# The output projection in half precision: high and low parts of both sides, one scale per 128 tokens

## The chip, the cores and the metric

One core of one Trainium2 chip runs the whole kernel. A core has five engines with queues of their own: TensorE (PE, matmuls into PSUM; its weight loads are shown apart as PEld), VectorE (DVE), ScalarE (ACT), GpSimd (POOL) and SyncE (SP, which here only issues transfers). Each works its queue in order; they wait for each other by semaphores. The metric is the time of one execution on the device in microseconds (us), as the median of several runs; lower is better.

## The reference

One decoder layer for 2048 tokens of width 1024 with two attention branches side by side. Only what matters here:

```python
proj = h @ w_in[l]                       # h: normalised, modulated x
qa, ka, va, fa, za, qb, kb, vb, zb = jnp.split(proj, split_points, axis=-1)
oa = forgetting_attention(qa, ka, va, fa + b_fgate[l])     # 8 heads of 64, causal
oa = oa * jax.nn.silu(za)
ob = sliding_window_sink_attention(qb, kb, vb, sinks[l])   # 8 heads of 64, window 128
ob = ob * jax.nn.silu(zb)
y = jnp.concatenate([oa, ob], axis=-1) @ w_out[l]          # (2048, 1024) @ (1024, 1024)
x = x + gate[:, None, :] * rms_norm(y, g_post[l])
```

The change is in the last matrix product, with `w_out` of 1024 x 1024, and in the normalisation behind it. A scale per token in front of the normalisation cancels in `y / rms(y)`, apart from the small constant under the root.

## The kernel before

The kernel keeps fp32 accuracy on a half-precision matrix unit by splitting: a number is written as a high part plus a low part, and a product takes three matmuls (high x high, high x low, low x high). The stages, in order of time:

1. Start: modulation vectors, first tiles of x, rotary tables.
2. Input projection, in units of three matmuls. A list of such units (`punits`) is worked off in small portions between the steps of the attention; tasks that belong to a certain unit hang in `events`.
3. The sliding-window branch (roughly 206 to 455 us): 64 windows, one per pair of heads and 128-token block. Each iteration of the loop over `windows` transposes the last window's probabilities (PE), takes exponentials (ACT), scores of the next window (PE), their maxima (DVE) and the product with the values (PE), with projection units in between.
4. The other branch ("fox"): 8 heads x 20 steps, each step with scores (PE), two exponentials (ACT), a low part (DVE) and the product with the values (PE). Inside the last head (`hd == 7`) the output projection is prepared: `open_out` makes room, `w_out_load` and `w_out_split` bring `w_out` in sixteen pieces and split each into a high part (ACT, L1247) and a low part (DVE, L1248), scaled by one factor per 128 rows (`facs`).
5. Output projection: 16 tiles of 128 tokens (`class Out`), the first two inside the last head, 14 after it.

One tile of stage 5: `load` brings the attention output (128 tokens x 1024) and the gate (`z`, kept transposed). `turn(h)` transposes four 128x128 blocks on PE into one PSUM bank (L1271), multiplies them by the gate on DVE (L1275), copies the result into a high part on ACT (L1276) and takes the low part on DVE (L1277). High and low parts of both sides are of type `F32R`, a four-byte format that PE multiplies in one pass. `product(n, k)` issues three matmuls for a half `n` of the 1024 columns and a block `k` of the 1024 rows (L1290); sixteen such units make a tile. When a half is complete, ACT sums its squares (`yj`, L1299) and DVE multiplies it by the gate vector (`yg`, L1300). After the second half, `store` makes the reciprocal root of the mean square with one-column operations on DVE (L1309, then L93 to L104), and a last product and sum over 128x1024 (L1312), and sends the tile out.

Two things set the order. `after(n, f)` puts `f` off by `n` ticks, and in stage 5 `tick2` makes a tick after every second unit. And PSUM: three banks, `bk`, are handed out in turn by `bank()`; a half of a tile holds one while it is summed, and the transposes take the others. The units of a tile, with the turns of the next tile between them:

```python
for q in range(16):
    ounits.append(lambda t=t, q=q: outs[t].product(q // 8, q % 8))
    if t + 1 < NB and q in (4, 7):
        ounits.append(lambda t=t, q=q: outs[t + 1].turn(int(q == 7)))
```

Of the kernel before, what the change touches and what calls it, by code (L numbers as in the profile page):

```python
# [11 lines left out]
F32R = mybir.dt.float32r  # L12
# [29 lines left out]
def hybrid_layer(  # L42
# [103 lines left out]
    snk = const.tile([P, 8], F32, name="snk")  # L146

# [101 lines left out]
    scl, isc, czs, facs, kaps = {}, {}, {}, {}, {}  # L249
# [4 lines left out]
    def w_done(key):  # L254

        kind, j = key[:2], key[2:]
        pw = pws[key]
        if kind == "qk":
            kap = kappa(pw, key)
            scl[key] = col(f"scl_{key}")  # L260
            V.tensor_scalar(scl[key][:], kap[:], kap[:], 0.125, op0=ALU.mult, op1=ALU.mult)
            isc[key] = col(f"isc_{key}")
            V.reciprocal(isc[key][:], scl[key][:])
        elif kind == "qb":
            kap = kappa(pw, key)
            scl[key] = col(f"scl_{key}")
            V.tensor_scalar(scl[key][:], kap[:], kaps["kb"][:], 0.125, op0=ALU.mult, op1=ALU.mult)
        elif kind == "va":
            kaps[key] = kappa(pw, key)
        else:  # L270
            czs[key] = col(f"cz_{key}")
            V.tensor_scalar(czs[key][:], pw[:], pH[:], 2.0 ** -29, op0=ALU.mult, op1=ALU.mult)
            facs[key] = col(f"fac_{key}")
            V.tensor_tensor(facs[key][:], kaps["vb" if kind == "zb" else f"va{j}"][:], czs[key][:], op=ALU.mult)
# [722 lines left out]
    with swa_order:  # L997
# [6 lines left out]
        ps_pv = swa_pool("ps_pv", 1, space=PSUM)  # L1004
        base = N_PRO
# [6 lines left out]
        for n, wd in enumerate(windows):  # L1012
# [14 lines left out]
            if n >= 2:  # L1027
                windows[n - 2].pv()
        windows[NW - 1].turn()
# [9 lines left out]
        tick()  # L1039
    swa.close()  # L1040
# [186 lines left out]
    def open_out():  # L1227
# [6 lines left out]
        oio["w"] = wo.tile([P, 2, KT, D], F32R, name="wohl")  # L1234
# [8 lines left out]
    def w_out_split(m):  # L1243
        k, cc = m // 2, slice((m % 2) * CH, (m % 2 + 1) * CH)
        fac = facs[f"za{k}" if k < 4 else f"zb{k - 4}"]
# [6 lines left out]
    class Out:  # L1252
# [13 lines left out]
        def turn(self, h):  # L1266

            px = bk[bank()][:].rearrange("p (k n) -> p k n", k=4)
            ks = slice(4 * h, 4 * h + 4)
            for k in range(4):  # L1270
                PE.transpose(px[:, k, :], self.o[:, (4 * h + k) * P:(4 * h + k + 1) * P], ident[:])  # L1271
            if h == 0:
                self.hl = [wpool.tile([P, KT, P], F32R, tag=tag, name=f"oz_{tag}") for tag in ("wraw", "whl")]
            hi, lo = self.hl[0][:, ks, :], self.hl[1][:, ks, :]
            after(1, lambda: V.tensor_tensor(self.z[:, ks, :], px, self.z[:, ks, :], op=ALU.mult))  # L1275
            after(2, lambda: A.activation(hi, self.z[:, ks, :], AF.Copy))  # L1276
            after(3, lambda: V.tensor_tensor(lo, self.z[:, ks, :], hi.bitcast(F32), op=ALU.subtract))  # L1277

        def product(self, n, k):
# [9 lines left out]
            for m_, (i, j) in enumerate(((0, 0), (0, 1), (1, 0))):  # L1289
                PE.matmul(py, self.hl[i][:, k, :], w_slot(8 * j + k)[:, cc],  # L1290
# [16 lines left out]
        def store(self):  # L1307
            ss, y = self.ss, self.y
            V.tensor_tensor(ss[:, 0:1], ss[:, 0:1], ss[:, 1:2], op=ALU.add)  # L1309
            rst = sm(1, "y_rs")  # L1310
            rsqrt_mean(rst, ss[:, 0:1], 1)
            V.scalar_tensor_tensor(y[:], y[:], rst[:], self.x[:], op0=ALU.mult, op1=ALU.add)  # L1312
            SP.dma_start(os_[self.t * P:(self.t + 1) * P, :], y[:])
# [13 lines left out]
    def ofill(n, each=None):  # L1327
        for _ in range(n):
            n_, q = divmod(opos[0], 18)
# [7 lines left out]
    with tc.manual_schedule():  # L1337
# [23 lines left out]
        for s, stp_ in enumerate(steps):  # L1361
# [4 lines left out]
            if hd == 7 and r >= 8:  # L1366
                npn, fil = N_IN * (r - 7) // (NS - 8) - opos[0], ofill
# [41 lines left out]
            if hd == 7 and r == 6:  # L1409
                outs[0].turn(0)  # L1410
                outs[0].turn(1)
# [52 lines left out]
```

## Time and profile before

| | |
|---|---|
| median of 3 runs | 1290.12 us (1289.17 to 1294.97) |
| profiled execution, its own time | 1293.69 us |
| its span, first to last instruction | 1292.0 us |
| mean granted PE clock | 0.98 |
| busy: PE, DVE, ACT, POOL | 1212.4, 925.5, 686.6, 156.7 us |

A row of the timeline or of the chain gives start and duration in us, engine, line of the kernel, operation, output<-inputs with partitions x elements and type; in brackets stands how long the engine had been idle before it and what released it. A row of the windows gives the stretch, its length, then for PE, PEld, DVE, ACT and POOL the busy time and the number of instructions, then the granted PE clock, the share of the transfer engines and GB/s. A group's row ends with busy time, mean ns of one, and idle time before. PE's matmuls are pipelined, so their durations overlap: what counts there is the distance from start to start.

### The profile page before, as it was taken

What the parts mean: (1) busy time and instruction counts of PE and PEld (TensorE: products, weight loads), DVE (VectorE), ACT (ScalarE), POOL (GpSimd) and SP (SyncE); (2) the same over time, 40 slices, a digit from 0 to 9 for tenths busy, and PEclk for the clock granted to TensorE, in tenths of its full rate; (3) what the DMA queues carried; (4) which work ended last, traced back from release to release, by engine and by line L of the source; (5) the groups of instructions that cost most, each with busy time, mean ns of one, the idle gap of its engine ahead of it and who ended that gap; (6) DMA issues with size and microseconds to landing.
All of it is one profiled execution on the core that took longest, in us unless ns stands there. A gap on an engine that the chain in (4) does not pass through costs nothing. (4 is left out here: it accounts for less than half of the span.)

```text
span 1292.0 us, 27969 instructions
## 1 busy us (share of the span) xinstructions
PE 1212.4 (94%) x11171; PEld 779.8 (60%) x11171; DVE 925.5 (72%) x2290; ACT 686.6 (53%) x1085; POOL 156.7 (12%) x284
## 2 busy tenths in 40 slices
PE   5788999999999999999999999999999969999997
PEld 2366545765558966555555555555555637777875
DVE  6666677686877637678878787877777886656655
ACT  2665435454545432666766676676767786322121
POOL 2001133233333310010010100000000000000000
PEclk9889999999999999999999999999999979999999
DMA  9345321213221322133142322122111154354442
GB/s 331 135 121 150 78 81 54 63 45 85 66 77 42 38 62 64 44 89 74 49 61 74 87 58 67 44 68 40 38 42 42 38 175 127 115 193 162 164 164 81
DMA packets 81909, 115.85 MB, mean 90 GB/s; under 512 B 26956, under 2 KB 57716, under 8 KB 81780
## 3 DMA queue, kind: packets, MB, share of 16 engines
q1 hardware_dynamic: 70292, 81.05, 20.6%
q0 software_dynamic: 11488, 33.03, 10.5%
q8 instruction: 87, 1.43, 0.5%
q14 instruction: 42, 0.34, 0.1%
HBM read 66.84 MB, written 25.18 MB: 71 GB/s over the span
## 5 line engine op out<-in xcount | busy, mean ns | idle before, releaser
L1124 DVE TENSOR_REDUCE a_m<-bk 128x1 f32<-128x512 f32 (+2 forms) x320 | 191.1, 606 | 102.0 <-PE bk L1120 68.9
L1173 ACT ACTIVATE p<-sta,lift,scl_qk 128x1024 f32<-128x1024 f32 (+2 forms) x160 | 171.9, 1075 | 94.7 <-DVE pha L1180 83.3
L294 PE MATMUL bk<-hT,wh_qk 128*128 128x512 f16 x768 | 201.8, 378 | 0.1
L1177 ACT ACTIVATE pha<-sta,lift,scl_qk 128x1024 f16<-128x1024 f32 (+2 forms) x160 | 171.7, 1073 | 0.9
L1180 DVE TENSOR_TENSOR pha<-p,pha 128x1024 f16<-128x1024 f32 (+2 forms) x160 | 168.8, 1055 | 0.7 <-ACT pha L1177 0.7
L1290 PE MATMUL bk<-wohl,oz_wraw 128*128 128x512 f32 x512 | 166.8, 407 | 0.2 <-DVE T L1275 0.2
L1120 PE MATMUL bk<-T 66*128 66x512 f16 (+2 forms) x320 | 111.8, 350 | 13.2 <-DVE a_m L1124 7.3
L1166 PE MATMUL sta<-T 128*128 128x512 f16 (+1 forms) x320 | 112.6, 352 | 7.5 <-ACT pha L1177 7.2
L1193 PE MATMUL poa<-vt,pha 128*128 128x65 f16 x1088 | 116.7, 193 | 1.3 <-DVE pha L1180 1.3
L1192 PE MATMUL poa<-vt,pha 128*128 128x64 f16 x1088 | 117.1, 195 | 0.0
L1190 PE MATMUL poa<-vt,pha 128*128 128x65 f16 x1088 | 117.1, 193 | 0.1
L1190 PEld LDWEIGHTS <-pha 128*128 128x128 f16 x1088 | 101.6, 97 | 20.1 <-issue 5.3
L294 PEld LDWEIGHTS <-wh_qk 128*128 128x128 f16 x768 | 70.5, 97 | 69.3 <-issue 2.6
L1167 PE MATMUL sta<-T 69*128 69x512 f16 (+1 forms) x320 | 111.3, 353 | 0.0
L1192 PEld LDWEIGHTS <-pha 128*128 128x128 f16 x1088 | 101.4, 97 | 15.0 <-issue 0.2
L1290 PEld LDWEIGHTS bk<-wohl,oz_wraw 128*128 128x128 f32 x512 | 93.5, 189 | 22.8 <-DVE T L1275 2.6
L294 PE MATMUL bk<-hT,wh_za 128*128 128x512 f16 x384 | 103.5, 378 | 0.9 <-DVE a_m L1124 0.9
L1193 PEld LDWEIGHTS <-pha 128*128 128x128 f16 x1088 | 101.5, 99 | 1.4 <-DVE pha L1180 1.4
L1290 PE MATMUL bk<-wohl,oz_whl 128*128 128x512 f32 x256 | 101.6, 397 | 0.0
L312 PE MATMUL bk<-wh_va,hT 128*128 128x128 f16 x1536 | 96.2, 219 | 1.1 <-issue 0.8
L294 PE MATMUL bk<-hT,wh_zb 128*128 128x512 f16 x384 | 93.7, 380 | 2.0 <-DVE wh_zb L238 2.0
L312 PEld LDWEIGHTS <-hT 128*128 128x128 f16 x1536 | 88.9, 98 | 9.9 <-issue 7.6
(649 smaller groups left out, 2067.1 us busy)
## 6 DMA issues: line engine op xcount, KB each, us to landing
wa<-in_w_ada_dram SPq DMA_DIRECT2D x16, 512.0 KB, 10.1
z_d<-tz POOLq DMA_DIRECT2D x32, 256.0 KB, 2.8
T<-stq SPq DMA_DIRECT2D x128, 64.0 KB, 2.0
T<-o_d SPq DMA_DIRECT2D x16, 512.0 KB, 5.0
T<-z_d SPq DMA_DIRECT2D x16, 512.0 KB, 5.7
xr<-in_x_dram SPq DMA_DIRECT2D x16, 512.0 KB, 4.2
out_dram<-yg SPq DMA_DIRECT2D x16, 512.0 KB, 3.0
xt<-in_x_dram SPq DMA_DIRECT2D x12, 512.0 KB, 7.3
```

The lines of the kernel that those rows point to most:

```text
L294: PE.matmul(ps, whl[:, a, k, :], hT[ci][:, b, k, :], start=(k == 0 and n == 0), stop=(k == KT - 1 and n == 2))
L312: PE.matmul(ps[:, u * P:(u + 1) * P], hT[ci][:, a, k, u * P:(u + 1) * P], whl[:, b, k, :], start=(k == 0 and n == 0), stop=(k == KT - 1 an ...
L1120: PE.matmul(mx[:, :w], T[0:XM, 0, i * P:(i + 1) * P], T[0:XM, 2, pc * CH:pc * CH + w], start=True, stop=pc < ci)
L1124: V.tensor_reduce(m3[:, u, pc:pc + 1], mx[:, :w], axis=AX.X, op=ALU.max)
L1166: PE.matmul(self.st[:, o:o + w], T[:, 3, kb_], T[:, 1, qc], start=True, stop=False)
L1173: A.activation(self.p32[:, :self.w], self.st[:, :self.w], AF.Exp, scale=scl[f"qk{self.hd}"][:], bias=lift[:])
L1177: A.activation(self.ph[:, 0, :self.w], self.st[:, :self.w], AF.Exp, scale=scl[f"qk{self.hd}"][:], bias=lift[:])
L1180: V.tensor_tensor(self.ph[:, 1, :self.w], self.p32[:, :self.w], self.ph[:, 0, :self.w], op=ALU.subtract)
L1190: PE.matmul(po[:, u, :], ph[:, 0, pq], vt[:, b, hd, 0:65], start=(self.first and n == 0 and u == 0), stop=False)
L1192: PE.matmul(po[:, u, 0:64], ph[:, 0, pq], vt[:, b, hd, 65:VW], start=False, stop=False)
L1193: PE.matmul(po[:, u, :], ph[:, 1, pq], vt[:, b, hd, 0:65], start=False, stop=(self.last and n == len(self.blocks) - 1))
L1290: PE.matmul(py, self.hl[i][:, k, :], w_slot(8 * j + k)[:, cc], start=(k == 0 and m_ == 0), stop=(k == KT - 1 and m_ == 2))
```

## The change

- Both sides of the output projection are kept as `F16` high and low parts in place of `F32R`; the three matmuls per unit stay.
- `F16` has a narrow range, so both sides get a scale. For each tile of 128 tokens it comes from the sum of squares of the gated, transposed tile: Square with a row sum on ACT (`squares_`), a matmul against ones on PE that adds over the partitions, and `root_scale`, two integer operations on DVE that make about a reciprocal root (`scale_`). High and low parts are then made of the whole tile at once with this scale.
- For `w_out` the sum of squares is taken during the windows of stage 3: each iteration loads a 128x128 block of `w_out` on SP's queue and squares the block of the iteration before on ACT; every 16th iteration, and at the end, DVE reduces. At the end of the stage a matmul against ones and `root_scale` give `wrt`. In `open_out` it is combined with the eight factors (now columns of `fac8`) into `wsc`, the scale of each 128 rows, and `ysc`.
- `store` takes the scales out again: four more one-column operations. The reciprocal root, for its part, has two operations in place of four in each of its three steps for a single column, and one more before them.
- A tile's eight transposes are issued together, into two banks, after the third product unit of the tile before, where they were two groups of four after the fifth and the eighth.
- Inside the last head the first tile's turn puts its scale off by three ticks, later tiles by four (`lag`); the products start one step later (r = 9), and a tile with a turn counts 17 units in place of 18.

The diff, cut to its core:

```diff
 def rsqrt_mean(dst, ss, n):
...
+        V.tensor_scalar(v[:], v[:], -0.5, None, op0=ALU.mult)
         for it in range(3):
             t = sm(n, "rs_t")
-            V.tensor_tensor(t[:], y[:], y[:], op=ALU.mult)
-            V.tensor_tensor(t[:], t[:], v[:], op=ALU.mult)
-            V.tensor_scalar(t[:], t[:], -0.5, 1.5, op0=ALU.mult, op1=ALU.add)
+            if n == 1:
+                V.scalar_tensor_tensor(t[:], y[:], y[:], v[:], op0=ALU.mult, op1=ALU.mult)
+            else:
+                V.tensor_tensor(t[:], y[:], y[:], op=ALU.mult)
+                V.tensor_tensor(t[:], t[:], v[:], op=ALU.mult)
             y2 = dst if it == 2 else sm(n, "rs_y")
-            V.tensor_tensor(y2[:], y[:], t[:], op=ALU.mult)
+            V.scalar_tensor_tensor(y2[:], t[:], 1.5, y[:], op0=ALU.add, op1=ALU.mult)
             y = y2
+
+    def root_scale(dst, ss):
+        h = small.tile([P, 1], I32, tag="rs_h", name="sc_h")
+        V.tensor_scalar(h[:], ss.bitcast(I32), 1, None, op0=ALU.logical_shift_right)
+        V.tensor_scalar(dst.bitcast(I32), h[:], -1, 0x5F3759DF + (15 << 23), op0=ALU.mult, op1=ALU.add)
...
# loop over the windows, at the end of iteration n
+            if n:
+                A.activation(wsq[n - 1][:], wsq[n - 1][:], AF.Square, accum_out=wss[:, (n - 1) % 16:(n - 1) % 16 + 1])
+            if n and n % 16 == 0:
+                V.tensor_reduce(wst[:, n // 16 - 1:n // 16], wss[:], axis=AX.X, op=ALU.add)
+            wsq[n] = wsp.tile([P, P], F32, tag="wsq", name="wsq")
+            SP.dma_start(wsq[n][:], w_out0[n // 8 * P:(n // 8 + 1) * P, n % 8 * P:(n % 8 + 1) * P])
...
# after the last window
+        A.activation(wsq[NW - 1][:], wsq[NW - 1][:], AF.Square, accum_out=wss[:, 15:16])
+        V.tensor_reduce(wst[:, 3:4], wss[:], axis=AX.X, op=ALU.add)
+        wsum = sm(1, "w_mx2")
+        V.tensor_reduce(wsum[:], wst[:], axis=AX.X, op=ALU.add)
+        pw_ = bk[bank()][:, 0:1]
+        PE.matmul(pw_, ones[:], wsum[:], start=True, stop=True)
+        root_scale(wrt[:], pw_)
...
-        oio["w"] = wo.tile([P, 2, KT, D], F32R, name="wohl")
+        oio["w"] = wo.tile([P, 2, KT, D], F16, name="wohl")
...
-        A.activation(hi, raw[:], AF.Copy, scale=fac[:])
-        V.scalar_tensor_tensor(w_slot(8 + k)[:, cc], raw[:], fac[:], hi.bitcast(F32), op0=ALU.mult, op1=ALU.subtract)
+        A.activation(hi, raw[:], AF.Copy, scale=wsc[:, k:k + 1])
+        V.scalar_tensor_tensor(w_slot(8 + k)[:, cc], raw[:], wsc[:, k:k + 1], hi, op0=ALU.mult, op1=ALU.subtract)
...
-        def turn(self, h):
...
+        def turn(self, lag):
+            px = [bk[bank()][:].rearrange("p (k n) -> p k n", k=4) for _ in range(2)]
+            for k in range(KT):
+                PE.transpose(px[k // 4][:, k % 4, :], self.o[:, k * P:(k + 1) * P], ident[:])
+            self.hl = wpool.tile([P, 2, KT, P], F16, tag="whl", name="oz")
+            self.sc = sm(1, "w_pw")
+            hi, lo = self.hl[:, 0], self.hl[:, 1]
+            gs = sm(1, "w_mx")
+
+            def gate():
+                for h in range(2):
+                    z = self.z[:, 4 * h:4 * h + 4, :]
+                    V.tensor_tensor(z, px[h], z, op=ALU.mult)
+
+            def squares_():
+                junk = wpool.tile([P, KT, P], BF16, tag="wraw", name="zj")
+                A.activation(junk[:], self.z, AF.Square, accum_out=gs[:])
+
+            def scale_():
+                pg = bk[bank()][:, 0:1]
+                PE.matmul(pg, ones[:], gs[:], start=True, stop=True)
+                root_scale(self.sc[:], pg)
+
+            after(1, gate)
+            after(2, squares_)
+            after(lag, scale_)
+            after(lag + 1, lambda: A.activation(hi, self.z, AF.Copy, scale=self.sc[:]))
+            after(lag + 2, lambda: V.scalar_tensor_tensor(lo, self.z, self.sc[:], hi, op0=ALU.mult, op1=ALU.subtract))
...
# store
+            inv = sm(1, "w_sw")
+            V.tensor_tensor(inv[:], self.sc[:], ysc[:], op=ALU.mult)
+            V.reciprocal(inv[:], inv[:])
             V.tensor_tensor(ss[:, 0:1], ss[:, 0:1], ss[:, 1:2], op=ALU.add)
+            V.tensor_scalar(ss[:, 0:1], ss[:, 0:1], inv[:], inv[:], op0=ALU.mult, op1=ALU.mult)
             rst = sm(1, "y_rs")
             rsqrt_mean(rst, ss[:, 0:1], 1)
+            V.tensor_tensor(rst[:], rst[:], inv[:], op=ALU.mult)
...
-            if t + 1 < NB and q in (4, 7):
-                ounits.append(lambda t=t, q=q: outs[t + 1].turn(int(q == 7)))
+            if t + 1 < NB and q == 2:
+                ounits.append(lambda t=t: outs[t + 1].turn(4))
...
-    N_IN = 2 * 18
+    N_IN = 2 * 17
...
             if hd == 7 and r >= 8:
-                npn, fil = N_IN * (r - 7) // (NS - 8) - opos[0], ofill
+                npn, fil = N_IN * (r - 8) // (NS - 9) - opos[0], ofill
...
             if hd == 7 and r == 6:
-                outs[0].turn(0)
-                outs[0].turn(1)
+                outs[0].turn(3)
```

More of the change, by code (lines that the diff above doesn't have):

```diff
@@ L11 @@
 F32 = mybir.dt.float32
-F32R = mybir.dt.float32r
 F16 = mybir.dt.float16
@@ L146, in hybrid_layer @@
     snk = const.tile([P, 8], F32, name="snk")
+    fac8 = const.tile([P, KT], F32, name="fac8")
+    wrt = const.tile([P, 1], F32, name="wrt")
+    wsc = const.tile([P, KT], F32, name="wsc")
+    ysc = const.tile([P, 1], F32, name="ysc")
     def kappa(pw, name):
@@ L248, in hybrid_layer @@
     pws = {}
-    scl, isc, czs, facs, kaps = {}, {}, {}, {}, {}
+    scl, isc, czs, kaps = {}, {}, {}, {}
     def col(name):
@@ L272, in w_done @@
             V.tensor_scalar(czs[key][:], pw[:], pH[:], 2.0 ** -29, op0=ALU.mult, op1=ALU.mult)
-            facs[key] = col(f"fac_{key}")
-            V.tensor_tensor(facs[key][:], kaps["vb" if kind == "zb" else f"va{j}"][:], czs[key][:], op=ALU.mult)
+            n = int(j) + (4 if kind == "zb" else 0)
+            V.tensor_tensor(fac8[:, n:n + 1], kaps["vb" if kind == "zb" else f"va{j}"][:], czs[key][:], op=ALU.mult)
     def pieces(key):
@@ L1004, in hybrid_layer @@
         ps_pv = swa_pool("ps_pv", 1, space=PSUM)
+        wsp = swa_pool("wsp", 2)
+        wss = swa_pool("wss", 1).tile([P, 16], F32, name="wss")
+        wst = sm(4, "wst")
+        wsq = {}
         base = N_PRO
@@ L1233, in open_out @@
         stp = foxo.enter_context(tc.tile_pool(name="stpo", bufs=3, reuse_waits="tile"))
-        oio["w"] = wo.tile([P, 2, KT, D], F32R, name="wohl")
+        oio["w"] = wo.tile([P, 2, KT, D], F16, name="wohl")
+        fm = sm(1, "w_p2")
+        V.tensor_reduce(fm[:], fac8[:], axis=AX.X, op=ALU.max)
+        V.reciprocal(fm[:], fm[:])
+        V.tensor_tensor(ysc[:], wrt[:], fm[:], op=ALU.mult)
+        V.tensor_scalar(wsc[:], fac8[:], ysc[:], None, op0=ALU.mult)
     w_raw = {}
@@ L1264, in load @@
             SP.dma_start(self.z, z_d[:, :, rows_].rearrange("k p n -> p k n"))
-        def turn(self, h):
[L1268 to L1277, printed above, removed]
+        def turn(self, lag):
[22 more added lines that the diff above has]
+            after(lag + 2, lambda: V.scalar_tensor_tensor(lo, self.z, self.sc[:], hi, op0=ALU.mult, op1=ALU.subtract))
         def product(self, n, k):
@@ L1289, in product @@
             for m_, (i, j) in enumerate(((0, 0), (0, 1), (1, 0))):
-                PE.matmul(py, self.hl[i][:, k, :], w_slot(8 * j + k)[:, cc],
+                PE.matmul(py, self.hl[:, i, k, :], w_slot(8 * j + k)[:, cc],
                           start=(k == 0 and m_ == 0), stop=(k == KT - 1 and m_ == 2))
@@ L1328, in ofill @@
         for _ in range(n):
-            n_, q = divmod(opos[0], 18)
+            n_, q = divmod(opos[0], 17)
             if q == 0 and n_ + 2 < NB:
```

1 line of the change is left out of this document (removed).

## The prediction

> **What bounds the kernel now.** I read the windows by stage first, then the chain that ended last, then the timeline of one 128-token tile of the output projection. The windows show TensorE (PE) busy nearly all the time in that last stage, at full clock, while ACT idles and DVE works 62% of it:
>
> ```profile
> 1180.00:1220.00 40.00, 39.80 (x182) 31.78 (x181) 24.92 (x73) 8.79 (x21) 0.00 (x0) 1.00 0.55 183
> ```
>
> So time is won where a tile's work on PE gets shorter, and lost where PE waits. From the chain, the first transpose group of six consecutive tiles:
>
> ```profile
> 1201.21 0.44 PE bk L1271 x4
> ...
> 1262.69 0.44 PE bk L1271 x4
> ```
>
> The two rows are five tiles apart: (1262.69 - 1201.21)/5 = 12.30 us a tile. One tile in the timeline:
>
> ```profile
> 1209.85 0.63 PE L1290 MATMUL bk<-wohl,oz_wraw 128*128 128x512 f32 x2
> ...
> 1210.83 0.69 DVE L1300 TENSOR_TENSOR yg<-bk,gacc 128x512 f32<-128x512 f32 x1 [2.70 <-ACT yj L1299]
> ...
> 1211.44 0.15 DVE L1309 TENSOR_TENSOR y_ss<-y_ss 128x1 f32<-128x1 f32 x1
> ...
> 1214.50 1.28 DVE L1312 SCALAR_TENSOR_TENSOR yg<-yg,y_rs,xr 128x1024 f32<-128x1024 f32 x1
> ...
> 1215.70 0.68 DVE L1275 TENSOR_TENSOR T<-bk,T 128x512 f32<-128x512 f32 x1
> ...
> 1216.44 0.30 PEld L1290 LDWEIGHTS bk<-wohl,oz_wraw 128*128 128x128 f32 x2 [0.19 <-DVE T L1275]
> ...
> 1216.47 0.64 ACT L1276 ACTIVATE oz_wraw<-T 128x512 fp32r<-128x512 f32 x1 [5.67 <-issue]
> ...
> 1217.01 0.39 PE L1290 MATMUL bk<-wohl,oz_whl 128*128 128x512 f32 x1
> ...
> 1221.91 0.39 PE L1290 MATMUL bk<-wohl,oz_whl 128*128 128x512 f32 x1
> ```
>
> Take the tile's first matmul, 1209.85, as time 0. DVE starts the previous tile's store at +1.59, needs 16 one-column operations until +4.65 (3.06/16 = 0.19 us each), then the 1.28 us row product, and only then, at +5.85, the first gating product (L1275) of the next tile: DVE runs in order, and the store stands ahead of it. PE already waits for that gating product, 0.19 us, since it holds the bank that the second half of columns needs. From 1217.01 to 1221.91 lie seven units of three matmuls: 0.70 us a unit, 0.233 a matmul. Sixteen units are 11.2 us; the other 1.1 are two groups of transposes and this wait.
>
> **The products in half precision.** The input projection's matmuls of the same 128x512 shape are already f16:
>
> ```profile
> 283.04 2.12 PE L294 MATMUL bk<-hT,wh_zb 128*128 128x512 f16 x9
> ...
> L294 PE MATMUL bk<-hT,wh_qk 128*128 128x512 f16 x768 | 201.8, 378 | 0.1
> ```
>
> Nine take 2.12 us, the last one's 0.38 included: (2.12 - 0.38)/8 = 0.217 each, 0.65 a unit. A tile's 48 save 48 x 0.016 = 0.8 us. That is all that the number format can bring, as products stay three. The Trainium skill ("TensorE: Matmul & The Clock Gate", Back-to-back issue gap) has about 131 ns for a sustained 512-column matmul in a stream with weight loads. By it a unit would be 0.39 us; the row of nine denies it, and the row decides.
>
> **Eight transposes at once** take the place of two groups of four, and stand after three units instead of five and eight. Twenty in a row:
>
> ```profile
> 44.41 2.35 PE L377 MATMUL px<-ident,xt 128*128 128x128 f32 x20
> ```
>
> A transpose more costs (2.35 - 0.3)/19 = 0.11 us; with the 0.44 of a group of four, eight cost 0.88, as much as two groups. Nothing is gained or lost there. With them a tile without waits is 16 x 0.65 + 0.9 = 11.3 us.
>
> **The scale per 128 tokens** adds a chain of four engines. Gate both halves (DVE), sum the squares of the whole tile (ACT), add over partitions with a matmul against ones (PE), two column operations (DVE), high part (ACT), low part (DVE). The matmul sits in PE's queue four ticks after the turn; a tick comes every second unit and a tile has 17, so it stands, tile about, after the ninth or the tenth product unit. All later units of the tile queue behind it, and DVE's next work behind its two column operations. When is its input ready?
>
> ```profile
> 42.44 1.06 ACT L359 ACTIVATE junk<-hT 128x1024 bf16<-128x1024 f32 x1
> 43.40 0.19 ACT L359 ACTIVATION_READ_ACCUMULATOR junk<-hT 128x1 f32 x1
> ...
> 47.97 0.38 PE L602 MATMUL bk<-bm,ones 1*128 1x1 f32 x2 [0.37 <-DVE bm L601]
> 48.28 0.10 PEld L294 LDWEIGHTS <-wh_kb 128*128 128x128 f16 x1
> 48.39 0.16 DVE L87 TENSOR_SCALAR p2t<-bk 128x1 f32<-128x1 f32 x1 [0.47 <-PE bk L602]
> ```
>
> The store keeps its length: four column operations are added for undoing the scales, five of the reciprocal root go, 15 instead of 16, and four of the 15 now read a column as their scalar, which is dearer (0.23 in the first row below against 0.15 for a plain one): the two roughly cancel. Store and gate fall in the same tick, store first, as before. So gating starts at +5.85 again; both halves are now issued together, the second 0.61 later (the step from 1210.83 to 1211.44), ending at +6.46 + 0.68 = +7.14. ACT follows 0.09 later (1216.38 to 1216.47): +7.23. The same Square over 128x1024 takes 0.96 until its accumulator is read, and 0.19 for that: +8.38, and with a handover PE starts the matmul at +8.45. Nearest row for it is the ones matmul L602: 0.31 until the next weight load, and about 0.1 until the products run at pace: 0.4. DVE reads its result 0.42 after its start (47.97 to 48.39).
>
> ```profile
> 49.34 0.23 DVE L609 TENSOR_SCALAR Gp<-gcol,ipH 128x8 f32<-128x8 f32 x1
> ...
> L232 ACT ACTIVATE wh_qk<-wr_qk,w_sw 128x1024 f16<-128x1024 f32 x8 | 9.1, 1141 | 2.6 <-DVE w_sw L224 1.6 <-PE bk L294 0.9
> ```
>
> PE, unhindered, would be there at 9 x 0.65 + 0.88 = +6.7, or +7.4 after ten units. So it waits 1.7 or 1.1 us in all (some of it already at the bank of the first gating product, free at +6.53). A tile then takes 8.45 + 0.4 + seven units (4.55) = 13.4, or with six units 12.75: mean 13.1, against 12.3. The saving of the format is spent and 0.8 us more. What follows the matmul is hidden: 0.4 until DVE has it and 0.4 for the scale, 1.14 high part, 1.28 low part end by about +12.8 with ACT's and DVE's other work between, and the next tile needs the low part only with its third matmul.
>
> The last stage holds 14 tiles, 13 of them with a turn: 13 x 0.8 = +10.4; the last tile has none and saves 0.8. After its last matmul the chain is the store's, 15 operations for 16: nothing. The two tiles worked off inside the last attention head save 96 x 0.016 = 1.5 and pay two ones matmuls, 0.8; starting them a step later moves their work by one unit. I take -0.7, from -3 to +2, since that stretch waits on several engines.
>
> **The scale for w_out** is summed in the sliding-window stage: per window a 64 KB load on SP's queue and a Square of 128x128 on ACT.
>
> ```profile
> sum 249.00, PE 246.63 PEld 167.23 DVE 180.81 ACT 124.40 POOL 82.76; mean PE 61.66 PEld 41.81 DVE 45.20 ACT 31.10 POOL 20.69
> L735 ACT ACTIVATE vb<-bk 128x128 f16<-128x128 f32 x16 | 3.5, 273 | 2.5 <-PE bk L727 2.4
> ...
> 303.22 0.19 ACT L829 ACTIVATION_READ_ACCUMULATOR sm__4001<-sm__4001,b_nb 128x1 f32 x1
> 303.31 0.57 ACT L847 ACTIVATE ptb<-pxb 128x512 f16<-128x512 f32 x1
> ...
> 307.03 0.64 PE L838 MATMUL pxb<-ident,sm__4001 128*128 128x128 f32 x4
> ...
> 307.25 0.68 DVE L843 TENSOR_TENSOR ptb<-pxb,ptb 128x512 f16<-128x512 f32 x1
> ...
> T<-stq SPq DMA_DIRECT2D x128, 64.0 KB, 2.0
> ```
>
> At 0.27 + 0.19 each, 64 add 30 us to ACT, which is busy 124 of the stage's 249 us; PE is busy 247. Behind the square in ACT's queue stand the next exponentials and copies; PE reads an exponential 3.6 us after ACT finished it (303.41 to 307.03) and DVE takes a copy 3.4 us after its end (303.88 to 307.25). A delay of 0.46 stays inside. A 64 KB load lands in 2.0 us and has a window of 3.9 us (249/64); SP's rotations queued behind it wait for ACT anyway. I take 0; 0 to +4, and 30 were the cover gone.
>
> Its end is exposed. A matmul against ones closes the stage in PE's queue, behind two DVE reductions that stand behind DVE's last evacuation:
>
> ```profile
> 463.68 0.62 PE L1087 MATMUL bk<-identh,lq 128*69 128x128 f16 x8
> ...
> 464.17 0.76 DVE L321 SCALAR_TENSOR_TENSOR vt<-bk,vt 128x256 f16<-128x256 f32 x2
> ```
>
> DVE is free at 464.93, the reductions take 0.4, the matmul 0.4: the first of the bias rows (L1087, now 463.68) starts near 465.8, and the row copies on ACT and the projections behind them move by 2.1 us.
>
> **Sum:** 10.4 - 0.8 - 0.7 + 2.1 = +11.0 us. The profiled execution took 1293.69 us for a span of 1292.0; so 1304.7 for such a one. The median of the runs is 3.6 lower, 1290.12: predicted 1301.1.
>
> **Rivals.** *The sum is there in time (faster).* The wait is gone if the squares are summed by +6.7 to +7.4 instead of +8.45, that is if DVE reaches the gating 1.7 us earlier. Against it: the order store, gate in DVE's queue, and 1215.70. For it: only that four of the one-column operations could run in DVE's gaps before +1.59, which program order forbids. Tiles of 11.7 (11.3 and the 0.4 matmul): -0.6 x 13 - 0.8 - 0.7 + 2.1 = -7.2, 1283. Chance 0.12, with 0.01 more for the 131 ns rule: tiles of 11.4 (8.45 + 0.4 + 6.5 x 0.39), 1279.
>
> *Half of it.* The chain is 0.4 to 0.8 us shorter, or the head saves its 3 us: +0 to +6, around 1293. Chance 0.18.
>
> *The clock falls.* PE idles 0.5 and then 1.2 us within two units. What idling did:
>
> ```profile
> 1038.80 0.38 PE L1166 MATMUL sta<-T 128*128 128x512 f16 x1 [1.84 <-ACT pha L1177]
> ...
> 1054.99 1.71 PE L1271 MATMUL bk<-ident,T 128*128 128x128 f32 x8 [2.24 <-DMA T<-o_d]
> ...
> 1056.49 0.63 PE L1166 MATMUL sta<-T 128*128 128x512 f16 x1
> ...
> 1055.00:1060.00 5.00, 3.81 (x13) 2.19 (x14) 2.15 (x4) 2.64 (x5) 0.00 (x0) 0.66 1.05 346
> ```
>
> After 1.84 us matmuls stayed at 0.38; after 2.24 they took 0.63, and the clock over 5 us was 0.66. Each such fall would cost some 2 us; in half the tiles that is +14, 1315. It decides from about 2 us of idling, and 1.2 is short of it: 0.06. The Trainium skill (same page, Part 1: The HAM clock gate) drops the clock after an idle window of about 3.4 us; by that rule this rival never comes, and the trace disagrees, with a fall after 2.24.
>
> **How the numbers follow.** The forecast, 0.63, spans 1296.6 to 1310 with the head's and the window stage's bounds. A measurement of this kernel can tell about 0.5%, 6.5 us: the forecast and the clock's case are slower, 0.69; the half case is the same, 0.18; the rest faster, 0.13. The range 1284 to 1310 leaves out the clock and most of the faster case.
>
> **What would show it.** In the profile after: units of 0.65 us; gating near +5.85, both halves together; Square at about +7.2; the ones matmul on PE waiting for ACT, 0.6 to 1.3 us, and a product waiting some 0.5 for the gate before it; periods alternating around 13.4 and 12.75; PE near full in the window stage; a wait of about 1.5 us at its end. I am wrong if PE meets the ones matmul without waiting, if tiles are under 12.3, if products keep 0.233, or if the window stage grows by more than 4 us.

## The result and the profile after

| | before | after |
|---|---|---|
| median of 5 runs | 1290.98 us (1289.17 to 1294.97) | 1302.61 us (1300.34 to 1305.98) |
| ratio, 95% interval | | 1.008 (1.006 to 1.010) |
| profiled execution, its span | 1293.69, 1292.0 us | 1300.34, 1298.6 us |
| last stage, second half of the second tile (the last inside the last head) to that of the last tile: 14 tiles | 173.5 us | 177.3 us |
| window stage, first to last value product | 281.2 us | 283.8 us |

The changed kernel is slower by about 0.8%. The two profiled executions lie only 6.6 us apart, one being above its median and the other below, so the stages are compared by their own rows and the total by the runs.

First the page of the kernel after: busy times and the groups of the product.

```profile
PE 1200.4 (92%) x11205; PEld 715.5 (55%) x11205; DVE 928.7 (72%) x2293; ACT 720.6 (55%) x1229; POOL 155.9 (12%) x284
...
L1342 PE MATMUL bk<-wohl,oz 128*128 128x512 f16 x768 | 176.3, 380 | 5.8 <-DVE T L1314 3.0
...
L1342 PEld LDWEIGHTS <-oz 128*128 128x128 f16 x768 | 74.3, 99 | 89.4 <-issue 6.9
```

PE is busy for 12.0 us less than before (1212.4) and the kernel is longer: PE waits. The view of PE's waits in the last stage says for what (us in all, times, longest):

```profile
PE bk L1322 <- ACT zj L1318: 8.3, 13, 1.0
PE bk L1342 <- DVE T L1314: 3.0, 12, 0.5
```

Thirteen times, once for each tile with a turn, PE waits at the ones matmul (L1322) for ACT's Square, and twelve times at the bank that the gate has not left yet. The timeline of one tile and of the start of the next (L1351 ends a half of columns, L1362 starts the store, L1369 ends it, L1314 is the gate, L1318 the Square, L1322 the ones matmul, L1342 the products):

```profile
1189.82 2.11 PE L1342 MATMUL bk<-wohl,oz 128*128 128x512 f16 x9
...
1190.08 0.60 ACT L1351 ACTIVATE yj<-bk 128x512 bf16<-128x512 f32 x1 [1.71 <-PE bk L1342]
...
1191.41 0.15 DVE L1362 TENSOR_TENSOR w_sw<-w_pw,ysc 128x1 f32<-128x1 f32 x1
...
1194.33 1.28 DVE L1369 SCALAR_TENSOR_TENSOR yg<-yg,y_rs,xr 128x1024 f32<-128x1024 f32 x1
1195.53 1.28 DVE L1314 TENSOR_TENSOR T<-bk,T 128x512 f32<-128x512 f32 x2
1196.27 0.81 PE L1342 MATMUL bk<-wohl,oz 128*128 128x512 f16 x3 [0.23 <-DVE T L1314]
1196.85 1.06 ACT L1318 ACTIVATE zj<-T 128x1024 bf16<-128x1024 f32 x1 [6.08 <-DVE T L1314]
1197.81 0.19 ACT L1318 ACTIVATION_READ_ACCUMULATOR zj<-T 128x1 f32 x1
...
1198.05 0.38 PE L1322 MATMUL bk<-w_mx,ones 128*128 128x1 f32 x2 [0.97 <-ACT zj L1318]
1198.29 6.63 PE L1342 MATMUL bk<-wohl,oz 128*128 128x512 f16 x30
...
1203.08 0.60 ACT L1351 ACTIVATE yj<-bk 128x512 bf16<-128x512 f32 x1 [3.09 <-PE bk L1342]
...
1211.04 0.38 PE L1322 MATMUL bk<-w_mx,ones 128*128 128x1 f32 x2 [0.33 <-ACT zj L1318]
...
1215.43 0.60 ACT L1351 ACTIVATE yj<-bk 128x512 bf16<-128x512 f32 x1 [1.71 <-PE bk L1342]
```

From 1189.82 the store starts at +1.59, the gate at +5.71, the Square at +7.03, the ones matmul at +8.23; products go on 0.24 later. The three ACT rows at L1351 are one tile apart: 13.00 and 12.35, alternating, 12.67 in the mean against 12.30 before. The last tile, with no turn, takes 10.36 against 11.19: the format's saving, as forecast.

### The profile page after: what moved, and what is told of

Its sections match the earlier page's. It is cut to its first block, busy times and chain, and to the rows that moved or that the text cites. A ratio compares the mean times of both kernels' runs of the same rounds, so it can differ in the third digit from the quotient of the medians.

```text
span 1298.6 us, 28342 instructions
## 1 busy us (share of the span) xinstructions
PE 1200.4 (92%) x11205; PEld 715.5 (55%) x11205; DVE 928.7 (72%) x2293; ACT 720.6 (55%) x1229; POOL 155.9 (12%) x284
## 4 chain that ended last, share of the span: by engine, by line
PE 64%; DVE 19%; DMA 7%; issue 5%; ACT 3%; SPq 1%; DVEq 0%; ACTq 0%
PE bk L306 25%; PE bk L1342 7%; PE bk L324 6%; PE bk L1150 4%; DVE a_m L1154 3%; PE sta L1196 3%; PE sta L1197 3%; DVE pha L1210 2%; PE pxb L850 2%; PE poa L1222 2%; PE pss L820 2%; PE poa L1223 2%; PE poa L1220 2%; DMA wo<-in_w_out_dram 2%; PE pob L868 2%
## 5 line engine op out<-in xcount | busy, mean ns | idle before, releaser
L1342 PE MATMUL bk<-wohl,oz 128*128 128x512 f16 x768 | 176.3, 380 | 5.8 <-DVE T L1314 3.0
L1342 PEld LDWEIGHTS <-oz 128*128 128x128 f16 x768 | 74.3, 99 | 89.4 <-issue 6.9
L324 PEld LDWEIGHTS <-hT 128*128 128x128 f16 x1536 | 88.9, 98 | 10.7 <-issue 8.5
L306 PE MATMUL bk<-hT,wh_qb 128*128 128x512 f16 x384 | 92.6, 380 | 0.0
```

The costliest lines, as they stand in the source:

```text
L306: PE.matmul(ps, whl[:, a, k, :], hT[ci][:, b, k, :], start=(k == 0 and n == 0), stop=(k == KT - 1 and n == 2))
L324: PE.matmul(ps[:, u * P:(u + 1) * P], hT[ci][:, a, k, u * P:(u + 1) * P], whl[:, b, k, :], start=(k == 0 and n == 0), stop=(k == KT - 1 an ...
L1342: PE.matmul(py, self.hl[:, i, k, :], w_slot(8 * j + k)[:, cc], start=(k == 0 and m_ == 0), stop=(k == KT - 1 and m_ == 2))
```

## The experiments

The **theory**: the ones matmul stands in PE's queue before the sum of squares can exist, because gate and Square stand behind the store on DVE; that costs over 1 us a tile, more than the format saves. The **rivals**: the format or the transposes bring nothing; or the cost lies in the sums for `w_out` during the windows. Each ratio is to the kernel before, timed on the same chip beside the runs of that row; rows that were not timed side by side differ by a few thousandths for the same kernel, and so little is not read. "Tile" is the usual distance from one second half to the next in the last stage (where two distances alternate, their mean); "tail" is the row on the last stage in the table above, and "window stage" is as there. Tile, tail and window stage come from one trace of each kernel.

| kernel | ratio (95%) | tile | tail | window stage |
|---|---|---|---|---|
| before | 1 | 12.30 | 173.5 | 281.2 |
| after_again: the changed kernel | 1.006 (1.004 to 1.008) | 12.67 | 177.3 | 287.6 |
| e0: half precision alone | 0.9934 (0.9910 to 0.9958) | 11.77 | 165.8 | 284.4 |
| e1: store behind the gate | 0.9952 (0.9935 to 0.9969) | 11.37 | 161.4 | 290.4 |
| e2: ones matmul a tick later | 0.9977 (0.9960 to 0.9994) | 11.76 | 165.6 | 285.2 |
| e3: no sums for `w_out` | 1.0008 (0.9988 to 1.0027) | 12.67 | 177.1 | 281.2 |
| e4: no scale per tile | 0.9935 (0.9911 to 0.9959) | 11.62 | 163.8 | 285.4 |
| e7: squares one window later | 1.0055 (1.0035 to 1.0076) | 12.67 | 177.3 | 285.3 |
| e5: e1 and e7 | 0.9960 (0.9943 to 0.9977) | 11.37 | 161.4 | 285.5 |
| e9: loads of the sums alone | 1.0086 (1.0066 to 1.0106) | 12.67 | 177.1 | 282.9 |
| e10: squares of the sums alone | 1.0087 (1.0065 to 1.0108) | 12.67 | 177.1 | 286.9 |
| e8: e1, sums in the other branch | 0.9958 (0.9940 to 0.9975) | 11.37 | 161.4 | 279.9 |

**after_again** is the changed kernel as it is, run beside others:

> The changed kernel, unchanged, timed beside the next three on one chip. Both theories: 1.008 of the kernel before. If the sums for w_out cost 3 us (theory) the kernel without them, at 1.0008, is not explained and this run would come out near 1.003; if they cost some 9 us (rival, from the run without them) it stays at 1.008.

It measured 1304.03 against 1296.66 us. The interval, 1.004 to 1.008, includes the rival's 1.008 and not the theory's 1.003. The kernel before took 1290.98 us in the first comparison and 1295.24 to 1296.66 beside the later ones, so only ratios are compared. The tail repeats to 0.1 us; the window stage came out 3.8 us longer than in the first profile. A single window stage is therefore not read closer than some 4 us.

**e0**, the kernel before with nothing but the format changed:

```diff
-        oio["w"] = wo.tile([P, 2, KT, D], F32R, name="wohl")
+        oio["w"] = wo.tile([P, 2, KT, D], F16, name="wohl")
...
-            after(2, lambda: A.activation(hi, self.z[:, ks, :], AF.Copy))
+            after(2, lambda: A.activation(hi, self.z[:, ks, :], AF.Copy, scale=2.0 ** -24))
```

> The kernel before with the F16 type alone: fixed powers of two (2^-24 for the tokens, 2^24 for w_out) in place of every scale, turns, store and order as before. It leaves out the scaling that the narrow range needs in general. Theory (a product costs 0.217 us in place of 0.233, but the gating behind the store holds a bank that PE needs): PE reaches that bank earlier and waits about 0.45 in place of 0.19 us, a tile takes 11.75 in place of 12.3, together with 1.5 in the last head 9 to 10 us less than before, near 1281.5. Rival (the format brings its full 0.78 us a tile): 12 us less, 1279. Rival (the format brings nothing, the pitch stays 0.233): 1291.

Timeline of e0, second halves of two tiles and a gate between them:

```profile
1196.80 0.60 ACT L1299 ACTIVATE yj<-bk 128x512 bf16<-128x512 f32 x1 [2.19 <-PE bk L1290]
...
1201.18 1.28 DVE L1312 SCALAR_TENSOR_TENSOR yg<-yg,y_rs,xr 128x1024 f32<-128x1024 f32 x1
...
1202.39 0.68 DVE L1275 TENSOR_TENSOR T<-bk,T 128x512 f32<-128x512 f32 x1
...
1203.12 0.59 PE L1290 MATMUL bk<-wohl,oz_wraw 128*128 128x512 f16 x2 [0.37 <-DVE T L1275]
...
1208.56 0.60 ACT L1299 ACTIVATE yj<-bk 128x512 bf16<-128x512 f32 x1 [2.19 <-PE bk L1290]
```

A tile of 11.76: 0.54 less than before, not 0.8, because the faster products arrive earlier at the gated bank and wait 0.37 us there in place of 0.19. The format's gain is real, 8.5 us in time, and part of it already ends at the store.

**e1**, one number: the store is put off by four ticks, so that gating stands ahead of it in DVE's queue.

```diff
-                after(3, self.store)
+                after(4, self.store)
```

> The changed kernel with one number changed: the store of a tile is put off by four ticks in place of three, so that it stands behind the next tile's gating in DVE's queue. Theory (PE waits for the ones matmul because the squares wait for the gating and the gating for the store): gating at about +2.9 us of a tile, squares summed near +5.5, PE arrives at +6.7 and does not wait; tiles of 11.55 in place of 12.68, 14 to 15 us less than the changed kernel, near 1288. Rival (the loss lies in the sums for w_out in the window stage): no difference, 1302. Rival (it is the added work itself, wherever it stands): no difference, 1302.

Timeline of e1:

```profile
1205.88 1.04 PE L1305 MATMUL bk<-ident,T 128*128 128x128 f32 x8
1206.52 1.29 DVE L1314 TENSOR_TENSOR T<-bk,T 128x512 f32<-128x512 f32 x2 [0.91 <-PE bk L1305]
1206.76 4.70 PE L1342 MATMUL bk<-wohl,oz 128*128 128x512 f16 x21
1207.84 1.06 ACT L1318 ACTIVATE zj<-T 128x1024 bf16<-128x1024 f32 x1 [2.95 <-DVE T L1314]
1208.81 0.19 ACT L1318 ACTIVATION_READ_ACCUMULATOR zj<-T 128x1 f32 x1
...
1210.65 1.28 DVE L1369 SCALAR_TENSOR_TENSOR yg<-yg,y_rs,xr 128x1024 f32<-128x1024 f32 x1
...
1211.29 0.28 PE L1322 MATMUL bk<-w_mx,ones 128*128 128x1 f32 x2
1211.43 5.99 PE L1342 MATMUL bk<-wohl,oz 128*128 128x512 f16 x27
```

The gate now starts while the last transposes run. The sum is there at 1209.00, 2.3 us before PE starts on it, and in this tile no row of PE has a wait. A tile is 48 x 0.216 + 0.88 + 0.14 = 11.39, measured 11.37. Both waits are gone, 15.9 us of the tail, and the kernel is faster than either of the two it came from. The theory holds for the last stage, in place and nearly in size (it had 14 to 15 us and tiles of 11.55).

**e2** leaves the store and moves the ones matmul, with the two steps behind it:

```diff
-                ounits.append(lambda t=t: outs[t + 1].turn(4))
+                ounits.append(lambda t=t: outs[t + 1].turn(5))
```

> The changed kernel with the ones matmul, and the high and low parts behind it, one tick (two product units, 1.3 us) later in the queues: lag 5 in place of 4. Theory: PE arrives at about +8.2 or +8.9, the sum is ready at +8.2, so the wait is gone; what is late next is the low part, which ends near +12.3 in every second tile and may hold the third matmul of the next tile by 0.4 us; tiles of 11.6 to 11.8, 11 to 13 us less than the changed kernel, near 1290.5. Rivals (window stage, or added work as such): no difference, 1302.

Timeline of e2:

```profile
1202.11 6.28 PE L1342 MATMUL bk<-wohl,oz 128*128 128x512 f16 x27
1203.69 1.28 DVE L1369 SCALAR_TENSOR_TENSOR yg<-yg,y_rs,xr 128x1024 f32<-128x1024 f32 x1
1204.89 1.28 DVE L1314 TENSOR_TENSOR T<-bk,T 128x512 f32<-128x512 f32 x2
...
1206.21 1.06 ACT L1318 ACTIVATE zj<-T 128x1024 bf16<-128x1024 f32 x1 [6.08 <-DVE T L1314]
...
1208.22 0.28 PE L1322 MATMUL bk<-w_mx,ones 128*128 128x1 f32 x2
```

The order store, gate, Square stays, with the Square at 1206.21; PE now comes two units later and does not wait in this tile. The 11.7 us that the tail wins are therefore the wait for the sum, apart from the one at the bank: the 27 products take 6.28, where 26 x 0.216 + 0.38 is 6.00, so some 0.3 us are still lost before the ones matmul. That is most of what divides this tile from e1's. The hold by the low part that was expected in every second tile is not seen: the tiles do not alternate.

**e4** takes the tile's Square, ones matmul and root away; high and low parts use a constant, so the scale no longer follows the data.

```diff
-            self.sc = sm(1, "w_pw")
+            self.sc = fsc
...
-            after(2, squares_)
-            after(lag, scale_)
-            after(lag + 1, lambda: A.activation(hi, self.z, AF.Copy, scale=self.sc[:]))
+            after(2, lambda: A.activation(hi, self.z, AF.Copy, scale=self.sc[:]))
...
```

> The changed kernel with a fixed power of two in place of the scale per 128 tokens: it leaves out the squares of the tile, the ones matmul and the two column operations; turn, store and order as they are. Theory: PE waits only for the gated bank, 0.35 us, as the store still stands ahead of the gating; tiles of 11.65 in place of 12.68, 13 us less than the changed kernel. Rival (the added work itself): the pieces left out are worth 0.25 us of PE a tile, 3 us less.

PE's waits of e4 in the last stage, first row:

```profile
PE bk L1342 <- DVE T L1316: 3.0, 12, 0.5
```

The wait for the sum is gone and the one at the bank stands as it was, 3.0 us in 12: they are two costs of the same arrangement, the store ahead of the gate. The ratio falls from 1.006 to 0.9935, some 16 us, where the theory had 13 and the rival 3. e1, which keeps the scale and changes the order, has the shorter tile (11.37 against 11.62). The scale itself is thus nearly free; its place was not.

**e3** sets the scale of `w_out` to a constant and leaves the loads, squares and reductions of the window stage out:

```diff
-            SP.dma_start(wsq[n][:], w_out0[n // 8 * P:(n // 8 + 1) * P, n % 8 * P:(n % 8 + 1) * P])
...
-        PE.matmul(pw_, ones[:], wsum[:], start=True, stop=True)
-        root_scale(wrt[:], pw_)
+        V.memset(wrt[:], 2.0 ** 15 / 32.0)
```

> The changed kernel with a fixed 1024 for the scale of w_out: the 64 loads, 64 squares, the reductions and the ones matmul at the end of the window stage are left out. Theory: the window stage gives back 2 us and its end 1 us, tiles stay at 12.68: 3 us less than the changed kernel, near 1299.5. Rival (the loss lies in these sums): all of the 11.6 us come back, 1291.

The ratio falls by 0.0052 from that of after_again and by 0.0072 from the first one: the sums cost some 7 to 9 us, with about 3.6 of uncertainty, over twice what the theory had. The total alone can't refute the rival: it would put e3 level with the kernel before, and 0.9988 to 1.0027 includes that. The rows refute it, since the tail keeps its 177.1 us without the sums. The window stage and what lies behind it, from the groups of the value product and of the first projections (count, ns, first and last start), of the kernel after and then of e3:

```profile
L868 PE MATMUL pob<-vb,ptb x744: 190/194/194, 180.2 to 464.0; 128*128 128x64 f16 x186
L306 PE MATMUL bk<-hT,wh_qk x768: 376/378/381, 468.7 to 984.7; 128*128 128x512 f16 x192
```

```profile
L868 PE MATMUL pob<-vb,ptb x744: 190/193/193, 177.9 to 459.1; 128*128 128x64 f16 x186
L306 PE MATMUL bk<-hT,wh_qk x768: 376/378/380, 463.0 to 979.0; 128*128 128x512 f16 x192
```

283.8 and 281.2 us for the stage, and 4.7 against 3.9 from its last value product to the first projection of the next. The tail is the same in both. What in the sums takes the time? The tile `wsq` of the kernel after, and PE's waits in its window stage:

```profile
its engine sat idle before it (us, times) until:
  DMA wsq<-in_w_out_dram: 31.2, 10
...
DMA to landing us min/median/max: 1.8/2.9/7.4
```

```profile
PE bk L324 <- issue: 1.6, 2, 1.2
PE pxb L850 <- ACT sm__3244 L841: 1.4, 1, 1.4
PE pxb L850 <- ACT sm__2247 L841: 1.2, 1, 1.2
```

Ten of the loads came so late that ACT stood 31.2 us for them, and twice PE waited for an exponential behind such a square. So a new theory: the loads are a window short of lead.

**e7** squares a block two windows after its load is issued instead of one. **e5** is e7 with e1's number.

```diff
-            if n:
-                A.activation(wsq[n - 1][:], wsq[n - 1][:], AF.Square, accum_out=wss[:, (n - 1) % 16:(n - 1) % 16 + 1])
...
+            if n >= 2:
+                w_square(n - 2)
```

> The changed kernel with each block of w_out squared two windows after its load in place of one: same loads, same squares, same buffers. Theory: in the profile ACT waited 31 us, in ten waits of up to 7.7, for these loads, and the exponentials behind them came late for PE; with a window more, 3.9 us, about half of the ten waits go and PE's waits for exponentials with them: 2 to 3 us less than the changed kernel. Rival (the window stage loses nothing, the loss is in the tiles alone): no difference. Rival (the sums cost 9 us, most of it by these waits): 5 to 8 us less.

> Both mends together: the store behind the next tile's gating (four ticks), and the squares two windows after the loads. If the two costs are separate they add: 16 us from the first (as measured against the kernel before) and 2 to 3 from the second: 0.993 of the kernel before, near 1287 where that takes 1295.7. If the window stage loses nothing: 0.995.

Tile `wsq` and PE's waits in the window stage of e7:

```profile
  DMA wsq<-in_w_out_dram: 3.9, 2
...
PE bk L324 <- issue: 2.6, 2, 1.3
PE pxb L850 <- issue: 2.2, 2, 2.0
```

ACT's waits fell from 31.2 to 3.9 us, PE's waits for exponentials are gone, and the time is the same: 1.0055 against 1.006, and e5 is no faster than e1. That theory falls. ACT had the slack, and what PE loses now has no releaser in the profile ("issue").

**e9** and **e10** halve the suspect: e9 issues the loads and doesn't square them, e10 squares the identity matrix and loads nothing. Either way the scale of `w_out` isn't that of the data.

```diff
 # e9
-                A.activation(wsq[n - 1][:], wsq[n - 1][:], AF.Square, accum_out=wss[:, (n - 1) % 16:(n - 1) % 16 + 1])
 # e10
-            SP.dma_start(wsq[n][:], w_out0[n // 8 * P:(n // 8 + 1) * P, n % 8 * P:(n % 8 + 1) * P])
```

> The changed kernel with the 64 loads of w_out in the window stage, but without the 64 squares (w_out has the fixed scale 1024; reductions and the ones matmul at the stage's end stay). Theory A (the squares hold ACT, by waiting for late loads and by their own 0.5 us, and the exponentials behind them come late): the stage is as short as without sums, 281 to 284 us from its first to its last value product, and the kernel near 1.001 to 1.002 of the kernel before. Theory B (the loads delay the rotations behind them in SP's queue and on the transfer engines): the stage stays at 285 to 288 and the kernel at 1.006.

> The changed kernel with the 64 squares on a tile that is always there, and without the 64 loads (fixed scale 1024 for w_out, so the sum leaves out w_out itself). Theory A1 (ACT's own 0.5 us per window is what costs): stage 285 to 288 us, kernel at 1.006. Theory A2 (the waits for late loads are what costs): stage 281 to 284, kernel near 1.002. Theory B (the loads in the queues): likewise near 1.002, so only the run with loads alone tells A2 from B.

1.0086 and 1.0087: by the totals each half costs as much as the whole did, and no theory fits both runs. The stage of e9 is 282.9 us, as theory A has it, with a total that theory A excludes; the stage of e10 is 286.9 and its total near 1.006, as theory A1 has it, but then the loads alone should have cost nothing. In e9 nothing reads the blocks, so its loads also run ahead of those of the kernel after: the last is issued at 418.3 us, there at 447.2.

The traces do show where the extra time of the stage stands. DVE reads the value product once in each of the 64 windows (L874; L862 before). From the 24th to the 56th of these reads every one of the thirteen traces, with or without sums, takes 140.3 us, to 0.1 us: there half of the loads and squares cost nothing. The 23 windows ahead take 100.4 to 104.9 us in the four kernels without sums and 102.0 to 109.0 in the nine with them, 3.6 more in the mean, and the eight behind 0.6 more. What PE loses there it loses at few places, most of them between 248 and 262 us and between 431 and 451 us; the kernels without sums have gaps there too. PE's gaps with no releaser add up to 1.5 to 3.4 us of the stage without sums and to 4.1 to 6.0 with them (1.6 in the first trace of the kernel after, and 2.7 behind late exponentials). Behind a longer one the clock can fall. In after_again (PE's timeline, then the windows):

```profile
255.12 0.19 PE L868 MATMUL pob<-vb,ptb 128*128 128x64 f16 x1 [2.49 <-issue]
...
255.00:260.00 5.00, 4.54 (x30) 2.20 (x30) 3.06 (x13) 1.99 (x8) 1.83 (x3) 0.69 0.10 28
```

In the first trace of the same kernel the clock over 255 to 260 us is 1.00, and its window stage is 3.8 us shorter. So the cost is not a price for each load or each square. What makes the gaps longer stays open, and rows that were not timed side by side (1.006 and 1.008 for the same kernel) may hide a part of it.

**e8** moves the sums, with e1's number, out of the windows into the heads of the other branch, as sixteen loads of 128x512 with a Square two steps after each:

```diff
+            ms, mr = divmod(s - 21, 6)
+            if 0 <= ms < 16 and mr == 0:
+                w_sum_load(ms)
+            if 0 <= ms < 16 and mr == 2:
+                w_sum_square(ms)
```

> The changed kernel with the store behind the next tile's gating (four ticks) and the sums for w_out moved: no loads or squares in the window stage; in the second attention stage every sixth step, from step 21 on, loads one of sixteen 128x512 pieces through the staging buffers and squares it two steps later, and one ones matmul follows. ACT gets 16 x 0.8 = 13 us in 500 us of which it idles about 30%. Theory: the window stage and its end give back their 4 to 5 us, tiles stay at 11.37, the attention stage hides the sixteen squares: 0.991 to 0.993 of the kernel before, 4 us less than with the later store alone (0.995). Rival (the sums cost the same wherever they stand): 0.995.

The same two groups of e8:

```profile
L868 PE MATMUL pob<-vb,ptb x744: 189/193/193, 182.6 to 462.5; 128*128 128x64 f16 x186
L306 PE MATMUL bk<-hT,wh_qk x768: 376/378/381, 466.4 to 991.0; 128*128 128x512 f16 x192
```

The window stage is back at 279.9 us and the step behind it at 3.9; but the stage that took the sums over has 524.6 us between its first and its last projection where the kernel after has 516.0. The total, 0.9958, is no better than e1's, as the rival had it. But the trace does not show a cost that follows the work: most of these 8.6 us is one event. The sixteen loads land in 2.7 to 10.7 us, 3.4 in the median, and the first is the slowest. ACT stands for it, PE stands for a copy that ACT has behind its square (L1264), and the granted clock falls over the next ten us:

```profile
611.31 0.63 ACT L1264 ACTIVATE ws<-ws 128x512 f32<-128x512 f32 x1 [5.30 <-DMA ws<-in_w_out_dram]
...
613.68 0.58 PE L1133 MATMUL bk<-T 66*128 66x512 f16 x1 [4.59 <-ACT T L1101]
...
610.00:615.00 5.00, 1.32 (x4) 0.48 (x4) 0.69 (x1) 3.64 (x6) 0.00 (x0) 0.61 1.00 227
615.00:620.00 5.00, 5.00 (x42) 2.93 (x41) 1.69 (x2) 1.72 (x4) 0.00 (x0) 0.71 0.00 1
```

By 629 us e8 is 6.8 us behind the kernel after in this stage. A first load with a longer lead was not run.

## Why the prediction was right, and where its steps were not

The forecast was slower by 11.0 us, 1301.1, against 1302.61 measured, and its likeliest case, the wait for the sum, is what came. The total agrees better than its terms: the largest was too large, and one that had been set to nothing was not.

**The chain in the tile** ran as written: the store at +1.59 as forecast, then gate, Square and ones matmul at +5.71, +7.03 and +8.23 where +5.85, +7.23 and +8.45 had been worked out; waits at the bank and at the ones matmul; two periods that alternate. Two sizes were off. The sum was ready 0.22 earlier: the fifteen column operations took 2.92 us (1191.41 to 1194.33) where sixteen before took 3.06, so dearer column scalars did not quite use up the operation saved, and ACT followed the gate after 0.04 and not 0.09. And the ones matmul held PE for 0.24 us, not 0.4. Together 0.38 a tile: 13.00 and 12.35 for 13.4 and 12.75, a tail of +3.8 us for +9.6. The rival "half of it" had named just such a chain, 0.4 to 0.8 us shorter; in the last stage it was nearer than the forecast.

**The window stage** had 0, with a bound of +4. Nine kernels with the sums or a half of them there show 285.9 us in the mean, the four without (before, e0, e3, e8) 281.7: about +4.2, the end of the range, from single values that spread over 282.9 to 290.4 and 279.9 to 284.4. The step that failed is the argument that a delay of 0.46 us in ACT's queue stays inside the slack of its readers. It let the square start on time: the landing of the loads had been taken as 2.0 us from another transfer, and was 2.9 in the median of the first trace and 2.0 in that of after_again, but 7.4 and 7.3 at most, and ten came late. That is the error in the reasoning; e7 shows that mending it brings no readable time back, so it is not shown to be the cause of the cost.

**The end of the window stage** had +2.1 and showed +0.8. The reduction and the ones matmul were there, but PE had the first bias rows ahead of them, so only a part stood open. **The last head** had -0.7 and shows +2.1 between the profiles (125.4 to 127.5 us from the last projection to the end of its second tile), within the spread of that stretch among kernels that are alike there (124.9 to 129.6 in after, after_again, e3, e7, e9 and e10).

So the tail's +3.8, the windows' +4.2, their end's +0.8 and the head's 0 to +2 make +9 to +11, beside measured ratios of 1.006 and 1.008, 7.8 and 10.3 us: a sum that came out through errors of opposite sign, so the closeness of the total is luck.

**The rivals.** "The sum is there in time" did not come by itself; e1 shows that its condition was the right one, as one tick for the store makes it true, and with it a faster kernel. The clock's case did not come in the last stage: the waits stay within 1.0 us, and the window over the last stage of the kernel after has a granted clock of 1.00 (the number after the five engines):

```profile
1118.00:1285.00 167.00, 155.73 (x764) 75.25 (x762) 102.14 (x301) 46.95 (x93) 0.00 (x0) 1.00 0.48 158
```

A fall of the clock did come in the window stage, where it falls in six of the thirteen traces, once or twice each, to 0.66 to 0.76 over five us. The limit of about 2 us of idling, which the prediction drew from two rows, is not borne out: in after_again the clock falls behind a gap of 2.49 us, and in e2 it stays at 1.00 behind one of 2.63 at the same place.

The products of this very stream run at (6.63 - 0.38)/29 = 0.216 us from start to start. The 131 ns that the Trainium skill ("TensorE: Matmul & The Clock Gate", Back-to-back issue gap) gives for a sustained stream of this width are not seen here either, with a weight load before each matmul and the weight loads hidden.

**Open:** what in the sums for `w_out` costs 7 us. ACT's waits for the loads are excluded as the main cause (e7), and by the totals loads alone and squares alone each cost as much as both (e9, e10). As far as the traces show it, the time stands in a few longer gaps of PE and not in every window, and most of these gaps have no releaser in the profile. One candidate that no run tests is the loading of instructions, which the page lists as a queue of its own (q8, 87 packets before and 88 after).

## What to carry to other kernels

Before a reduction is put between two products, list what stands ahead of its first input on every engine it passes: here a store that nobody waited for stood ahead of a gate that everybody waited for, and one tick turned a loss of 0.6 to 0.8% into a gain of 0.5%. Cost a new wait by when its input is ready, not by the work added; the scale for each tile, with its Square, ones matmul and root, cost PE 0.14 us once it had its place. And a sum that comes out right is no proof of its terms: compare them stage by stage with the profile after.

## What was not expected of the hardware

A wait on an in-order engine that is not the bound can be large and nearly free: ACT stood 31.2 us for 64 KB loads, and taking 27 of them away changed nothing readable (1.0055 against 1.006). It need not be: in e8 one such wait of 5.30 us reached PE as 4.59 us, and the clock over the ten us behind it was 0.61 and 0.71. The 64 KB loads landed in 1.8 to 7.4 us on the same queue in the same stage. The ones matmul's row shows 0.38 us, but it delays the products by 0.24 where it was waited for (1198.05 to 1198.29) and by 0.14 where it was not (1211.29 to 1211.43 in e1). And the view of waits understates what waits cost: the two rows of the kernel after add up to 11.3 us, of which e1 keeps 0.5, yet e1's tail is 15.9 us shorter. Each stop also breaks PE's overlap, and a 0.38 us product that would have passed on after 0.216 is waited out. As an estimate, 25 stops at 0.16 us and 13 ones matmuls that hold PE 0.10 us longer make 5.4 us, beside the 5.1 that the two rows leave over.
